# First head first in two attentions, small roots on GpSimd, a reordered opening, and whole-width blocks in the last feed-forward

## The chip, the cores and the metric

The kernel runs on one core of one Trainium2 chip. A core has five engines that run their own instruction lists side by side and wait for one another on semaphores: TensorE (PE, matrix multiplication, with its weight loads shown apart as PEld), VectorE (DVE), ScalarE (ACT), GpSimd (POOL) and SyncE (SP), which here issues nearly all transfers. Each engine works through its list in order. Matmul results go to PSUM, everything else lies in SBUF. The metric is the device time of one execution in microseconds.

## The reference

A backbone of two layers works on 512 latent tokens and 256 context tokens of width 1024, all in float32. In each layer a modulation vector (the "ada" products) scales and shifts the RMS norm of the tokens; one large projection feeds four mixers: A, attention in a window of tokens plus the context, B, dense attention with RMS-normed queries and keys, C, a gated recurrence in chunks (mLSTM), and D, a state-space scan in chunks (Mamba). Their outputs are projected back and added, and a feed-forward with squared relu follows. The last layer does not need the context's outputs.

```python
def attend(qblk, keys, vals, mask=None, sink=None):
    s = jnp.einsum('bqgrd,bkgd->bgrqk', qblk, keys)
    ...
def sq_relu_ffn(h, w1, w2):
    return jnp.square(jax.nn.relu(h @ w1)) @ w2
...
        x = x + gt1 * (jnp.concatenate([ya, yb, ym, yd], axis=-1) @ w_out[layer])
        h2 = rmsnorm(x, g_norm2[layer]) * (1 + sc2) + sh2
        x = x + gt2 * sq_relu_ffn(h2, w_ff1[layer], w_ff2[layer])
    return rmsnorm(x, g_final)
```

## The kernel before, in words

**Precision by splitting.** Each float32 operand of a large product is split into a rounded part and a remainder (h and hl, wh and wl, ah and al, yh and yl): ACT writes the rounded part, DVE the remainder, and three matmuls (high by high, high by low, low by high) make one product. The DVE and ACT work of most stages is this splitting. Line 96 is the helper of all plain matmuls, L107 of DVE's two-operand operations, L104 of ACT's, L112 and L115 of DVE's with scalars.

**Order of the work.** Latents are tokens 256 to 767 (LAT, 512 columns), the context the first 256 (CTX). The function walks through a layer stage by stage: projections, attention A, D, C, attention B, output projection, feed-forward. Stages of narrow or dependent matmuls are interleaved with wide ones by a stream of generators: `fill(t)` advances the stream by some work, and tables of numbers (FILL_A, FILL_D, FILL_C, FILL_CB) say how much stands at which place. A scheduler then orders each engine's instructions by when their inputs are modelled to be ready, so the order on an engine is not that of the program text. Tiles come from pools with a fixed number of buffers, and a new tile waits until the old one in its buffer is read.

**Opening (layer 0).** SP loads the tokens x in four pieces with constants (cst), per-column and per-row tables (pcol, prow) in between. ACT squares x, PE sums over partitions (ssq), four transposes and nine small DVE steps (`rsq`, a reciprocal root by a bit trick and two refinements) give the norm; PE spreads it to a row (prow_), ACT copies that to SBUF (rowx), and `norm_chunk` multiplies x by it (xn). `cond(q)` loads and multiplies the ada weights of the next columns; the wopen weights then feed the first projections.

**Attention.** `put_k` makes for each of two key heads a tile KHL with the rounded keys in one half of the partitions and the remainder in the other, for both: ACT rounds, DVE subtracts, DVE copies the rounded half across and ACT the remainder. `put_q` makes the query tiles EO, `rotate` applies the rotary embedding with two POOL multiplications and one on DVE (qs, ra), `v_ab` splits the values. `attend_s` makes the scores (tile s) of one unit, a key head and 128 queries, `attend_v` the products with the values. A has 12 units in layer 0 and 8 in layer 1, all of head 0 first. B in layer 0 does four query blocks of head 0, the same of head 1, then the other two; in layer 1 the heads alternate with each query block.

**Stage C and the start of B.** For each 128 tokens C makes raw products, an exponential mask (MB), the inter product with the state, the num product with the values (65 columns wide), and a norm over each head: ssC holds the squares' sums, `c_norm` takes their roots on DVE, `c_fin` multiplies on POOL (tho) and transposes. The stream at that time holds the projections of B's keys and queries: their squares (bsq) are summed by 2-column matmuls (`col_b`), `rsq_b` takes roots on DVE, `apply_k` multiplies the keys. For the last two blocks of tokens the norm and `c_fin` fall together with B's KHL and EO.

**Feed-forward.** Eight blocks b: `ffn1(b)` makes 512 hidden features, `ffn2(b - 1)` multiplies those of the block before back to 1024 and adds them to x. In layer 1 only the 512 latents count. Their inputs h2 are not normed: the two halves of 256 tokens are finished at different times, the norm's row is multiplied on DVE after the matmul, and two extra columns carry the shift (bs). So every product of `ffn1` is done in two parts, of 258 and 256 columns.

## Time and profile before

| | |
|---|---|
| median of 3 runs | 1825.8 us (1821.95 to 1827.46) |
| profiled execution | 1831.02 us |
| its span on the core | 1829.2 us |
| mean granted clock of TensorE | 0.981 |
| instructions | 31114 |
| POOL busy | 330.4 us, 332 instructions |
| bytes moved by the queue that the engines' transfers use | 176.88 MB |

A group of the profile names line, engine and operation, then the tile written, the tiles read, shapes and count, busy time and mean of one, and the idle time just before with the instruction that ended it. In the list of single instructions each row starts with time and duration, and the idle time before it stands in brackets. In the table by stretch of time the busy time of each engine is followed by the clock that the TensorE was granted (1.00 is full), the share of the DMA engines and GB/s.

### The profile page before, as it was taken

The page shows a single profiled execution, that of the slowest core. Times are in us where ns is not written, and L with a number is a line of the kernel's source. Part 1 is how long each engine was busy: PE and PEld are TensorE (multiplying, and loading weights), DVE is VectorE, ACT ScalarE, POOL GpSimd, SP SyncE. Part 2 cuts the span into 40 slices and gives each one's busy share as a digit, 9 for nine tenths or more (in the row PEclk, how much of TensorE's full clock was granted, in tenths as well). Part 3 has the DMA queues.
Part 4 walks back from the last instruction along what each step waited for, and adds up shares of the span by engine and source line. Part 5 has one row for each costly group of instructions (what it writes and reads, how often), then busy time and mean ns, then how long its engine had stood idle before and what let it go on. Part 6 is the DMA issues. An engine that isn't in the chain of part 4 may idle for free. (4 is left out here: it accounts for less than half of the span.)

```text
span 1829.2 us, 31114 instructions
## 1 busy us (share of the span) xinstructions
PE 1756.3 (96%) x11754; PEld 1541.2 (84%) x11754; DVE 1167.8 (64%) x2601; ACT 896.5 (49%) x1988; POOL 330.4 (18%) x332
## 2 busy tenths in 40 slices
PE   7999999989999999999999999999989999999997
...
GB/s 336 89 82 110 147 139 95 91 121 41 24 82 112 96 132 103 95 127 98 99 127 98 139 70 61 47 94 93 70 58 70 35 105 92 93 93 93 94 96 65
DMA packets 97685, 178.85 MB, mean 98 GB/s; under 512 B 10624, under 2 KB 19200, under 8 KB 97536
## 3 DMA queue, kind: packets, MB, share of 16 engines
q1 hardware_dynamic: 97536, 176.88, 30.1%
...
q14 instruction: 57, 0.47, 0.1%
...
## 5 line engine op out<-in xcount | busy, mean ns | idle before, releaser
L104 ACT ACTIVATE wh<-wraw 128x512 fp32r<-128x512 f32 (+1 forms) x392 | 238.4, 618 | 257.1 <-PE bulk L96 136.4
L107 DVE TENSOR_TENSOR wl<-wraw,wh 128x512 fp32r<-128x512 f32 (+1 forms) x392 | 281.9, 725 | 116.9 <-ACT wh L104 108.6
L96 PE MATMUL s<-h,wh 128*128 128x258 f32 (+2 forms) x1040 | 316.2, 313 | 1.1 <-ACT pr L104 1.1
L96 PE MATMUL s<-hl,wh 128*128 128x258 f32 (+2 forms) x1040 | 306.2, 313 | 0.0
L96 PE MATMUL s<-h,wl 128*128 128x258 f32 (+2 forms) x1040 | 252.5, 313 | 0.0
L96 PE MATMUL bulk<-ah,wh 128*128 128x512 f32 (+1 forms) x576 | 218.0, 378 | 3.9 <-DVE mod L107 3.2
L302 POOL TENSOR_TENSOR acc<-acc,adap 128x512 f32<-128x512 f32 x96 | 143.2, 1496 | 412.1 <-ACT acc L104 390.6
L96 PE MATMUL bulk<-ah,wl 128*128 128x512 f32 (+1 forms) x576 | 216.1, 375 | 0.0
L96 PE MATMUL bulk<-al,wh 128*128 128x512 f32 (+1 forms) x576 | 215.9, 375 | 0.0
L96 PEld LDWEIGHTS s<-h,wh 128*128 128x128 f32 x1040 | 197.0, 189 | 22.4 <-ACT pr L104 1.6
L115 DVE SCALAR_TENSOR_TENSOR x<-bulk,mod,x 128x512 f32<-128x512 f32 (+1 forms) x224 | 149.4, 671 | 103.3 <-PE bulk L96 102.2
L96 PEld LDWEIGHTS s<-hl,wh 128*128 128x128 f32 x1040 | 197.5, 190 | 11.8 <-issue 0.4
L96 PEld LDWEIGHTS s<-h,wl 128*128 128x128 f32 x1040 | 166.1, 190 | 1.1
L96 PE MATMUL bulk<-h,wh 128*128 128x512 f32 (+1 forms) x416 | 154.0, 370 | 3.8 <-DVE VS L107 2.3
L96 PE MATMUL bulk<-hl,wh 128*128 128x512 f32 (+1 forms) x416 | 144.8, 348 | 0.0
L96 PE MATMUL bulk<-h,wl 128*128 128x512 f32 (+1 forms) x416 | 144.5, 347 | 0.0
L96 PEld LDWEIGHTS bulk<-ah,wh 128*128 128x128 f32 x576 | 108.3, 188 | 24.9 <-DVE mod L107 4.9
L96 PEld LDWEIGHTS bulk<-ah,wl 128*128 128x128 f32 x576 | 108.2, 188 | 21.2
L96 PEld LDWEIGHTS bulk<-al,wh 128*128 128x128 f32 x576 | 108.3, 188 | 19.4
L104 ACT ACTIVATE relu<-relu,bs 128x512 f32<-128x512 f32 x96 | 58.8, 644 | 131.1 <-DVE relu L107 131.1
L104 ACT ACTIVATE adap<-adar,silw 128x256 f32<-128x256 f32 x192 | 85.2, 497 | 56.9 <-DMA adar<-in_wada_dram 52.6
L107 DVE TENSOR_TENSOR relu<-relu 128x512 f32<-128x512 f32 x96 | 88.1, 943 | 31.4 <-ACT relu L104 31.3
...
## 6 DMA issues: line engine op xcount, KB each, us to landing
wraw<-in_wf_dram SPq DMA_DIRECT2D x256, 256.0 KB, 2.7
...
```

Of the source, the lines that this page charges most:

```text
L96: return TE.matmul(o, lhsT=l, rhs=r, start=start, stop=stop)
L104: return S.activation(o, i, f, scale=scale, **kw)
L107: return V.tensor_tensor(o, a, b, op)
L115: return V.scalar_tensor_tensor(o, a, s, b, op0, op1)
L302: G.tensor_tensor(acc[:, v], acc[:, v], dst, ALU.add)
```

## The change

The change has six parts.

*Opening.* The four pieces of x are sent first, then cst and pcol; the first ada weights and wopen's first piece follow, the row tables and layer 1's pcol after them. The first two normalised chunks read the norm's row from PSUM, and its copy to SBUF comes behind them.

*First head first.* `put_k` takes a list of heads. In layer 0's A keys and queries of head 0 are rotated and split first; the values, head 1 and the context's queries follow. In B head 1's keys and queries follow the first unit. In layer 1 B's units alternate between the heads in pairs of query blocks. Where an attention has no scores made ahead, the same amount of stream work as behind the first scores also goes ahead of them.

*Copy by DMA.* For head 1 one POOL DMA copies rounded part and remainder across partitions instead of DVE and ACT.

*Roots on POOL.* `rsq` can run on POOL: eleven steps there, and the bit trick on DVE. C's norm and the norms of B's keys and queries use it; the last two `c_fin` multiply on DVE.

*Stage C.* The 2-column sums and the roots behind them wait in a list (mids) until the middle of the stream's next wide group. Both directions' weighted values (vw) are made before a common piece of stream work. The inter product directly follows raw, and a piece of stream work stands between the two halves of num.

*Feed-forward, layer 1.* While block 1 starts, `whole()` makes the normed latents in one piece: POOL multiplies x by the row, ACT scales and shifts, and the second 256 columns are split into h2's free columns; the first 256 follow at block 2. Blocks 2 to 7 then use 512-column matmuls, and the relu reads PSUM directly.

```diff
-    def load_cols(l):
-        SY.dma_start(pcs[l], pcol[l])
+    def load_row(l):
...
-        if q == 1:
-            SY.dma_start(cs, cst)
-        if q == 2:
-            load_cols(0)
+    SY.dma_start(cs, cst)
+    SY.dma_start(pcs[0], pcol[0])
...
-    def rsq(out_, src, scale, eps):
+    def rsq(out_, src, scale, eps, eng=V):
...
+        eng.tensor_scalar(v, src, scale, eps, ALU.mult, ALU.add)
         ts(y.bitcast(I32), v.bitcast(I32), -0.5, float(0x5F3759DF), ALU.mult, ALU.add)
...
+        eng.tensor_tensor(w, y, y, ALU.mult)
+        eng.tensor_tensor(w, w, v, ALU.mult)
+        if eng is V:
...
+        eng.tensor_scalar(t, w, -10.0 / 3.0, None, ALU.add)
+        eng.tensor_tensor(w, w, t, ALU.mult)
+        eng.tensor_scalar(w, w, 5.0, None, ALU.add)
+        eng.tensor_tensor(y, y, w, ALU.mult)
+        eng.tensor_tensor(w, y, y, ALU.mult)
+        eng.tensor_tensor(w, w, v, ALU.mult)
+        eng.tensor_scalar(w, w, -0.5 * 0.375 ** 3, 1.5 * 0.375, ALU.mult, ALU.add)
+        eng.tensor_tensor(out_, w, y, ALU.mult)
...
+            todo = mids.pop(0) if mids else None
             for k in range(len(W)):
+                if todo is not None and k == len(W) // 2:
+                    todo()
...
+            raws0 = [ada_load(i, (4, 0)[i]) for i in range(2)]
...
+            cond(0, raws0)
+            W0 = wload([wopen[i, 0] for i in range(2)])
+            for l_ in range(DEPTH):
+                load_row(l_)
+            SY.dma_start(pcs[1], pcol[1])
...
+                if q == 0:
+                    act(rows[i], prows[i], AF.Copy)
...
+        def put_k(src, khl_, sl, bs=(0, 1)):
+            for b in bs:
                 own = slice(64 * b, 64 * b + 64)
                 oth = slice(64 - 64 * b, 128 - 64 * b)
                 H, L = khl_[b][:, 0, sl], khl_[b][:, 1, sl]
                 act(H[own], src[own], AF.Copy)
                 tt(L[own], src[own], H[own].bitcast(F32), ALU.subtract)
-                V.tensor_copy(H[oth], H[own].bitcast(F32))
-                act(L[oth], L[own].bitcast(F32), AF.Copy)
+                if b:
+                    G.dma_start(khl_[b][oth, :, sl], khl_[b][own, :, sl])
+                else:
+                    V.tensor_copy(H[oth], H[own].bitcast(F32))
+                    act(L[oth], L[own].bitcast(F32), AF.Copy)
...
+            f = (stream.total - (first if head else 2 * first) - last) / nf
+            if head is None:
+                fill(first)
...
-            v_ab(pav[1], 0, 2)
-            put_k(pf[1][:, 0:256], khl["A"], CTX)
-            q_a(0, CTX, pf[1][:, 256:512])
-            put_k(rotate(pf[0][:, 0, :], None, tf((P, NL), name="ra"), rp), khl["A"], LAT)
-            q_a(0, LAT, pf[0][:, 1, :])
+            rk = rotate(pf[0][:, 0, :], None, tf((P, NL), name="ra"), rp)
+            put_k(pf[1][:, 0:256], khl["A"], CTX, (0,))
+            rq0 = rotate(pf[0][:, 1, :], None, tf((P, NL), name="ra"), rp)
+            put_k(rk, khl["A"], LAT, (0,))
+            put_q(rq0, eos["A", 0], LAT)
             for i in range(2):
                 v_ab(pav[0][:, i, :], 2 + 2 * i, 2)
+            v_ab(pav[1], 0, 2)
+            put_k(pf[1][:, 0:256], khl["A"], CTX, (1,))
+            put_k(rk, khl["A"], LAT, (1,))
+            q_a(0, CTX, pf[1][:, 256:512])
...
+                rsq(v, v, 1.0 / 64.0, EPS, G)
...
+        def later(*fs):
+            return g_do(lambda: mids.append(lambda: [f() for f in fs]), 0.4 * len(fs))
...
+        def cq(m):
+            return later(*[col_b(f"q{m}", sl, sqq) for sl in segs_q], rsq_b(f"q{m}", jq))
+
+        gs = [later(*[col_b("k", sl, sqk) for sl in (LAT, CTX)], rsq_b("k")), gq(0, LAT)]
+        gs += [gq(0, CTX)] if need else []
+        gs += [cq(0), g_do(apply_k(LAT), 0.5), g_do(apply_k(CTX), 0.5), gq(1, LAT)]
+        gs += [gq(1, CTX)] if need else []
+        gs += [cq(1)]
...
+                vws.append(vw)
+            fill(2 * wu * fC_)
+            for d in range(2):
+                j, vw = ORDERS[d][st], vws[d]
...
+            rsq(ssC[:, t4], ssC[:, t4], 1.0 / 64.0, EPS, G)
...
+            inter = s2()
+            for e in range(2):
+                for q in range(2):
+                    er = slice(64 * e, 64 * e + 64)
+                    mm(inter[:, e, q * 130:(q + 1) * 130], qT[er, q, js], SC[er, :, j, q, :])
...
+            fill((wa + 0.6 * wb) * fC_ if ji < nout - 1 else 1.5 * FILL_CB[l][4])
             num = s2()
             for e in range(2):
+                if e:
+                    fill(0.4 * wb * fC_ if ji < nout - 1 else 0.5 * FILL_CB[l][4])
...
-            put_k(kB[:, sl], khl["B"], sl)
+            put_k(kB[:, sl], khl["B"], sl, (0,))
...
+        for sl in segs_out:
+            put_q(qB[:, 0, sl], eos["B", 0], sl)
+        units = [(kv, j) for js_ in ((out_tok[:4], out_tok[4:]) if need else (out_tok[:2], out_tok[2:])) for kv in range(2) for j in js_]
...
+            c_fin(j, V)
...
         def done_b(kv, j):
+            if (kv, j) == units[0]:
+                for sl in (LAT, CTX):
+                    put_k(kB[:, sl], khl["B"], sl, (1,))
+                for sl in segs_out:
+                    put_q(qB[:, 1, sl], eos["B", 1], sl)
...
+        def whole():
+            for c in range(8):
+                t = T((P, NL), F32, "ada", 4, "xn") if c % 2 == 0 else ta((P, NL), name="xn")
+                nrm.append(t)
+                G.tensor_tensor(t, xr[c // 2][:, c % 2, LAT], rowt[0], ALU.mult)
+                act(t, t, AF.Identity, scale=sc2[0][:, c:c + 1], bias=md[:, 0, 24 + c:25 + c])
+                put_whole(c, 1)
+
+        def put_whole(c, i):
+            dst = slice(NE + 256 * i, NE + 256 * i + 256)
+            split_act(nrm[c][:, 256 * i:256 * i + 256], h2[c][0][:, dst], h2[c][1][:, dst], slice(0, 256))
...
+            full = not need and b >= 2
...
+                sg = [(0, slice(NE, NE + NL))] if full else psegs
+                if full:
+                    ks = [(m, [0], k) for m in range(2) for k in range(8)]
...
+                    if full:
+                        act(r[:, LAT], o[:, 0, :], AF.Relu)
+                        tt(r[:, LAT], r[:, LAT], r[:, LAT], ALU.mult)
+                        split_act(r[:, LAT], ah, al, LAT)
+                        continue
...
+            if not need and b == 1:
+                whole()
+            if not need and b == 2:
+                for c in range(8):
+                    put_whole(c, 0)
```

The scheduler's order shows where it moves instructions. SP in the opening (x, cc, cst are tokens, condition and constants, adaw and wraw weights), before:

```order
L133 DMA x_66<-in_xin_dram 128x1536
L137 DMA cst_63<-in_cst_dram 128x386
L133 DMA x_67<-in_xin_dram 128x1536
L129 DMA pcol_69<-in_pcol_dram 128x102
L130 DMA prow_71<-in_prow_dram 128x40
L133 DMA x_68<-in_xin_dram 128x1536
L232 DMA adaw_189<-in_wada_dram 128x1024
L232 DMA adaw_199<-in_wada_dram 128x1024
L232 DMA adaw_216<-in_wada_dram 128x1024
L232 DMA adaw_226<-in_wada_dram 128x1024
```

and with the change:

```order
L132 DMA x_66<-in_xin_dram 128x1536
L132 DMA x_67<-in_xin_dram 128x1536
L132 DMA x_68<-in_xin_dram 128x1536
L135 DMA cst_63<-in_cst_dram 128x386
L136 DMA pcol_69<-in_pcol_dram 128x102
L241 DMA adaw_101<-in_wada_dram 128x1024
L241 DMA adaw_103<-in_wada_dram 128x1024
L241 DMA adaw_105<-in_wada_dram 128x1024
L241 DMA adaw_107<-in_wada_dram 128x1024
L176 DMA wraw_241<-in_wopen_dram 128x512
L176 DMA wraw_247<-in_wopen_dram 128x512
L129 DMA prow_71<-in_prow_dram 128x40
```

The constants and the first pcol now stand behind the fourth x, the row table prow behind the first ada and wopen weights.

DVE at the start of A in layer 0 (KHL_797 is head 0's keys, KHL_798 head 1's, EO_799 head 0's queries, ra rotated tiles, VS values), before:

```order
L107 TENSOR_TENSOR ra_829<-s_56_186,rope_793 128x512
L107 TENSOR_TENSOR VS_796<-s_54_184,VS_796 128x2x2x64
L107 TENSOR_TENSOR EO_799<-bulk_187,EO_799 64x256 x2
L107 TENSOR_TENSOR KHL_797<-ra_829,KHL_797 64x512
L628 CAST KHL_797<-KHL_797 64x512
L107 TENSOR_TENSOR KHL_798<-ra_829,KHL_798 64x512
L628 CAST KHL_798<-KHL_798 64x512
L107 TENSOR_TENSOR ra_846<-s_56_186,rope_793 128x512
L107 TENSOR_TENSOR wl_1021<-wraw_1026,wh_1020 128x280
L107 TENSOR_TENSOR EO_799<-ra_846,EO_799 64x512 x2
```

and with the change, where KHL, EO and VS keep their numbers:

```order
L107 TENSOR_TENSOR ra_813<-s_60_191,rope_793 128x512
L107 TENSOR_TENSOR KHL_797<-bulk_192,KHL_797 64x256
L659 CAST KHL_797<-KHL_797 64x256
L107 TENSOR_TENSOR VS_796<-s_58_189,VS_796 128x2x2x64
L107 TENSOR_TENSOR wl_994<-wraw_999,wh_993 128x280
L107 TENSOR_TENSOR ra_826<-s_60_191,rope_793 128x512
L107 TENSOR_TENSOR KHL_797<-ra_813,KHL_797 64x512
L659 CAST KHL_797<-KHL_797 64x512
L107 TENSOR_TENSOR KHL_798<-bulk_192,KHL_798 64x256
L107 TENSOR_TENSOR EO_799<-ra_826,EO_799 64x512
L107 TENSOR_TENSOR KHL_798<-ra_813,KHL_798 64x512
L107 TENSOR_TENSOR EO_799<-ra_826,EO_799 64x512
```

Head 1's two copies (CAST) are gone, its splits stand behind head 0's keys, and the second rotation (the queries') comes ahead of head 0's latent keys.

DVE at the start of B in layer 0, from the last sum of C's norm (ssC) on (rv, ry, rw are steps of its root, KHL_4863 is head 1's keys, EO_4880 and EO_4881 are head 0's queries; head 0's keys stand farther ahead), before:

```order
L1385 TENSOR_REDUCE ssC_4053<-sqc_4788 128x4
L107 TENSOR_TENSOR KHL_4863<-kB_3671,KHL_4863 64x512
L112 TENSOR_SCALAR rv_4792<-ssC_4053 128x8
L628 CAST KHL_4863<-KHL_4863 64x512
L112 TENSOR_SCALAR ry_4793<-rv_4792 128x8
L107 TENSOR_TENSOR KHL_4863<-kB_3671,KHL_4863 64x256
L107 TENSOR_TENSOR rw_4794<-ry_4793 128x8
L628 CAST KHL_4863<-KHL_4863 64x256
L107 TENSOR_TENSOR rw_4794<-rw_4794,rv_4792 128x8
L107 TENSOR_TENSOR EO_4880<-qB_3672,EO_4880 64x512
L115 SCALAR_TENSOR_TENSOR rw_4794<-rw_4794 128x8
```

and with the change (rg is the root's tile on POOL, m the maximum of the first scores, EO_4875 and EO_4876 head 0's queries):

```order
L1429 TENSOR_REDUCE ssC_4051<-sqc_4790 128x4
L107 TENSOR_TENSOR EO_4875<-qB_3670,EO_4875 64x256
L112 TENSOR_SCALAR rg_4794<-rg_4794 128x8
L107 TENSOR_TENSOR EO_4876<-qB_3670,EO_4876 64x256
L107 TENSOR_TENSOR wl_4979<-wraw_4980,wh_4978 128x512
L721 TENSOR_REDUCE m_916_4886<-s_918_4888 128x1
L721 TENSOR_REDUCE m_916_4886<-s_920_4897 128x1
L115 SCALAR_TENSOR_TENSOR m_916_4886<-m_916_4886,rq_792 128x1
L1376 TENSOR_TENSOR tho_3668<-tho_3668,ssC_4051 128x256
L115 SCALAR_TENSOR_TENSOR m_916_4886<-m_916_4886,rq_792 128x1
L115 SCALAR_TENSOR_TENSOR x_4646<-bulk_4829,mod_89,x_4646 128x512
L1376 TENSOR_TENSOR tho_3668<-tho_3668,ssC_4051 128x256
```

Of the root one step is left on DVE; head 1's splits stand farther behind, and the multiplications of tho (L1376) with additions to x behind them have come to DVE.

92 lines of the change are left out of this document (35 added, 57 removed).

## The prediction

> **What bounds the kernel now.** I read the page first, for the busy shares:
>
> ```profile
> PE 1756.3 (96%) x11754; PEld 1541.2 (84%) x11754; DVE 1167.8 (64%) x2601; ACT 896.5 (49%) x1988; POOL 330.4 (18%) x332
> ```
>
> TensorE (PE) is the bound, and the other engines matter where they stop it. Two things can be gained: time in which PE stands still, and time in which it works slowly. The table by stretch of time shows both; the columns are busy time of PE, PEld, DVE, ACT, POOL, then the granted clock.
>
> ```profile
> 28.00:84.00 56.00, 55.94 (x530) 48.66 (x531) 30.75 (x73) 31.29 (x70) 11.71 (x10) 0.97 0.47 155
> 84.00:94.00 10.00, 6.24 (x26) 4.97 (x25) 7.08 (x12) 7.71 (x16) 5.18 (x4) 0.66 0.36 108
> 320.00:364.00 44.00, 43.19 (x286) 35.82 (x286) 26.32 (x75) 20.02 (x48) 11.64 (x13) 0.84 0.31 95
> 364.00:394.00 30.00, 29.12 (x206) 24.69 (x205) 22.98 (x67) 15.99 (x29) 8.68 (x9) 0.83 0.43 138
> 394.00:412.00 18.00, 12.01 (x58) 9.59 (x57) 15.65 (x37) 8.91 (x23) 2.39 (x3) 0.81 0.24 79
> 1320.00:1354.00 34.00, 32.98 (x195) 27.02 (x194) 27.29 (x79) 20.70 (x39) 9.26 (x9) 0.95 0.23 71
> 1354.00:1376.00 22.00, 15.24 (x58) 11.41 (x58) 20.04 (x54) 9.35 (x23) 3.59 (x5) 0.84 0.23 79
> 1498.50:1771.00 272.50, 272.50 (x1730) 247.15 (x1729) 148.03 (x242) 90.83 (x145) 0.00 (x0) 1.00 0.30 94
> ```
>
> From such a row I take two upper bounds: standing time, the length less PE's busy time, and clock loss, the length times (1 − clock). 84 to 94 (A's start in layer 0): 3.8 and 3.4. 320 to 394 (stage C, layer 0): 1.7 and 12.1. 394 to 412 (B's start, layer 0): 6.0 and 3.4. 1320 to 1354 (C, layer 1): 1.0 and 1.7. 1354 to 1376 (B's start, layer 1): 6.8 and 3.5. Clock loss counts idle time too, so the two overlap. From 1498 on PE is full at full clock; only less work shortens that.
>
> **The feed-forward of layer 1.** The chain of waits alternates blocks of the first product (tile s) with blocks of the second (bulk):
>
> ```profile
> 1520.60 23.16 PE s L96 x192
> 1543.76 22.30 PE bulk L96 x96
> 1566.05 23.16 PE s L96 x192
> 1589.21 22.20 PE bulk L96 x96
> 1747.58 23.12 PE s L96 x192
> ```
>
> Both do the same arithmetic, but the first as 192 matmuls of 256 and 258 columns, since the two halves of the tokens are normalised at different times and each half carries extra columns. The change gives blocks 2 to 7 a finished 512-column input, so they become 96 matmuls of 512 columns, the bulk form: 23.15 − 22.25 = 0.9 us each, six blocks, **−5.6 us** (−5 to −6). The relu then reads PSUM without the row multiplication, so DVE has less to do.
>
> The price is the new input. Right after block 0's inputs, POOL multiplies eight 128x512 tiles, ACT shifts and rounds them, DVE takes the rest. POOL's nearest rows:
>
> ```profile
> L302 POOL TENSOR_TENSOR acc<-acc,adap 128x512 f32<-128x512 f32 x96 | 143.2, 1496 | 412.1 <-ACT acc L104 390.6 <-ACT adap L104 18.6
> L606 POOL TENSOR_TENSOR qs<-qs,rope 128x512 f32<-128x512 f32 x12 | 15.7, 1306 | 142.5 <-ACT qs L104 142.5
> L1333 POOL TENSOR_TENSOR tho<-tho,ssC 128x256 f32<-128x256 f32 x10 | 7.1, 731 | 23.6 <-DVE ssC L115 23.6
> L1013 POOL MEMSET v<- 128x24 f32 x2 | 0.3, 142 | 44.1 <-PE s L96 44.1
> ```
>
> Eight at 1.31 to 1.50 us are 10.5 to 12.0 us, and ACT, in order, follows them. Queued behind on ACT is block 1's weight rounding, needed for these matmuls:
>
> ```profile
> L104 ACT ACTIVATE wh<-wraw 128x512 fp32r<-128x512 f32 (+1 forms) x392 | 238.4, 618 | 257.1 <-PE bulk L96 136.4
> 1461.08 0.39 ACT L104 ACTIVATE row<-mx 128x256 f32<-128x256 f32 x1 [4.46 <-PE mx L96]
> 1475.06 0.29 PE L96 MATMUL s<-h,wh 128*128 128x258 f32 x1
> ```
>
> The row exists at 1461.5, so POOL is through at 1472.0 to 1473.5, and ACT's last pair plus the first weights (0.62 + 0.39 + 0.62) land at 1473.6 to 1475.1, against a need at 1475.1. Bounds 0 and +3 (if DVE's subtractions queue too); I take **+1.0**. The second half of this input is rewritten under a 22 us bulk block by 8 × 0.39 = 3.1 us of ACT and as much of DVE: nothing.
>
> **The opening.**
>
> ```profile
> 4.00:8.00 4.00, 1.87 (x8) 0.40 (x8) 0.59 (x4) 2.43 (x4) 0.00 (x0) 1.00 1.03 403
> 8.00:12.00 4.00, 4.00 (x17) 0.75 (x16) 0.51 (x4) 2.41 (x4) 0.00 (x0) 1.00 0.66 244
> 14.43 1.57 ACT L104 ACTIVATE sq<-x 128x768 f32<-128x768 f32 x2 [1.73 <-DMA x<-in_xin_dram]
> 24.67 0.87 ACT L104 ACTIVATE rowx<-s 128x512 f32<-128x512 f32 x2 [2.29 <-PE s L96]
> 25.30 1.42 DVE L115 SCALAR_TENSOR_TENSOR xn<-x,sc,rowx 128x512 f32<-128x512 f32 x2 [1.87 <-ACT rowx L104]
> 28.06 0.39 PE L96 MATMUL s<-wh,h 128*128 128x256 f32 x1 [1.71 <-ACT h L104]
> ```
>
> Constants and two tables of small packets stand ahead of the fourth x, and the transfers sag from 403 to 244 GB/s in 8 to 12 us. The change sends all four x first: at 403 GB/s the 159 GB/s missing for 4 us are 1.6 us, and cst (0.2 MB) is 0.5. x then lands 2.1 us sooner, more if the weights behind it also share less. The normalisation multiplies straight from PSUM (0.63 us of copying off the path), and the row's matmuls go ahead of an ada transpose (some 0.7). The first projection moves by 3.4 or more; afterwards PE has no idle to absorb it (55.94 of 56 us). Bounds −1.6 (all that follows tied to the transfers) and −5; I take **−3.5**.
>
> **Attention A.** Before, both heads' keys were split, copied across partitions by DVE and ACT, and the values split too, ahead of the first scores:
>
> ```profile
> 82.72 0.63 ACT L104 ACTIVATE KHL<-KHL 64x512 fp32r<-64x512 f32 x1
> 88.17 1.22 PE L96 MATMUL s<-KHL,EO 128*128 128x512 f32 x2 [3.76 <-DVE EO L107]
> 1120.87 0.50 PE L96 MATMUL s<-KHL,EO 128*128 128x512 f32 x1 [1.50 <-DVE EO L107]
> ```
>
> Layer 0 now rotates keys and queries first, prepares head 0 alone, and sends head 1's copy by two POOL DMAs. On ACT head 1's rounding and its copy, 0.63 each, no longer stand between the query's rotation and its split, and the values' splits, about as long together, partly move behind too: 2.5 of the 3.8 us, and with so short a stall 1.5 of the 3.4 us of clock loss. Bounds −1 (POOL's part of the rotation, 2 × 1.31, stays) and −7.2 (both whole); I take **−4.0**. In layer 1 the prologue gets an equal filling before the first scores, taken out of later ones: **−1.2**, bounds 0 and −1.5. Head 1's copy has many attention units before its first reader.
>
> **Stage C.** Here PE hardly stands but is slowed:
>
> ```profile
> 345.00:349.90 4.90, 4.45 (x40) 4.31 (x38) 2.60 (x7) 4.78 (x13) 3.38 (x5) 1.00 0.11 28
> 349.90:360.10 10.20, 10.20 (x39) 7.60 (x38) 5.72 (x14) 3.56 (x12) 2.85 (x4) 0.50 0.21 52
> 373.80:384.00 10.20, 9.60 (x58) 7.32 (x58) 8.78 (x31) 6.19 (x13) 1.50 (x1) 0.50 0.79 252
> 348.39 1.05 PE L96 MATMUL bulk<-cst,bsq 128*128 128x2 f32 x8 [0.45 <-DVE qB L115]
> ```
>
> Half clock comes after runs of narrow matmuls (2 and 65 columns) with stalls below 1 us. The change hangs the 2-column sums into the middle of a wide group, moves the inter products up and puts wide work between the halves of num. That may cost one window of 10.2 us, worth at most 5.1, or none. Bounds +2 (narrow runs meet elsewhere) and −8; I take **−2.5** for both layers.
>
> The Trainium skill, "TensorE: Matmul & The Clock Gate", section "Why this matters for your kernels", asks for no PE-idle gaps over about 3 us. By it breaking narrow runs wins nothing, and only the 3.76 us stall matters. The trace disagrees: the window at 349.9 follows no such gap. By the rule the sum is 2.5 us smaller, which the third rival contains.
>
> **Attention B.** Layer 0, where DVE runs the root of C's norm (9 steps) and the eight key and query splits in turn, and PE waits for all of it:
>
> ```profile
> 396.58 0.17 DVE L112 TENSOR_SCALAR rv<-ssC 128x8 f32<-128x8 f32 x1
> 397.24 0.17 DVE L112 TENSOR_SCALAR ry<-rv 128x8 int32<-128x8 int32 x1
> 402.47 0.17 DVE L115 SCALAR_TENSOR_TENSOR ssC<-rw,ry 128x8 f32<-128x8 f32 x1
> 399.45 1.87 PE L96 MATMUL s<-KHL,EO 128*128 128x384 f32 x8 [1.00 <-DVE EO L107]
> 403.88 0.44 PE L1336 MATMUL mx<-cst,tho 128*128 128x128 f32 x2 [1.97 <-POOL tho L1333]
> 407.50 0.58 PE L96 MATMUL bulk<-yh,wh 128*128 128x256 f32 x1 [2.18 <-DVE x L115]
> ```
>
> The root takes 402.64 − 396.58 = 6.1 us there. After the change head 1's splits come after the first unit, and the root is 11 steps on POOL with one on DVE. No row has a small arithmetic step on POOL. Below: MEMSET 128x24, 0.14 us; above: tho 128x256, 0.73. From 128x256 to 128x512 a multiplication grows by 0.58 us; taken back to 24 elements that leaves 0.21, near the MEMSET. I take 0.21: 12 × 0.21 + 0.2 for two changes of engine = 2.7 us, 3.4 less than now. New wait: DVE's multiplication of tho waits for POOL, and behind it in DVE's order stand additions to x that free PE's PSUM. With about 3 us of DVE work between, that wait is short. Head 1's copies (POOL DMAs) are read several units later in layer 0, two in layer 1.
>
> Of the 6.0 us standing and the half clock after it I take **−4.0** in layer 0 and **−4.0** in layer 1 (6.8 standing), each with bounds +3 (the 0.73 step) and −8. Roots for k and q go to POOL likewise, under wide feature groups.
>
> The Trainium skill, "GPSIMD Engine Reference", section "Key points", holds VectorE structurally about twice as fast at elementwise work. By that, twice DVE's 0.17, the root would take 12 × 0.34 = 4.1 us instead of 2.7, and the gain in B would shrink by some 1.4 us in each layer. No run shows it yet.
>
> **Sum.** −5.6 + 1.0 − 3.5 − 4.0 − 1.2 − 2.5 − 4.0 − 4.0 = −23.8. The profiled execution took 1831.0 us: 1807.2. It lies 5.2 above the median of 1825.8, so at the median 1802.0. Some waits will move rather than vanish: I leave 2 us for that and forecast **1804 us**.
>
> **Rivals.** *Only the firm parts land* (0.22). Feed-forward (−4.6 with its price) and opening (−3.5) count, A by half (−2.6); C and B find new waits as long as the old: −10.7, 1815. For it: DVE is busy 15.65 of 18 us in B's start and the work is only reordered. Against: 6 us of standing there comes from an order that the change undoes.
>
> *POOL's roots become the bound* (0.06), the slower side. With steps of 0.73 us a root is 12 × 0.73 = 8.8 us. It decides from 6.1 / 12 = 0.5 us a step, where it takes longer than today's. At 0.73, B loses its 8.0 and pays 2.7 a layer: +13.4. Three roots a layer for k, q0 and q1 grow from 9 × 0.17 = 1.5 to 8.8, by 7.3; a half feature group (12 matmuls of 22.3 / 96 = 0.23, 2.8) covers part, 4.5 stays, times six +27. 1804 + 13 + 27 = 1844; with four of the six covered, 1826, and with three 1831. Against: the sizes are 2 to 16 elements, not 256.
>
> *The clock stays low* (0.12). Stalls go, but the narrow runs and a shorter stall still halve the clock: C's 2.5 and the clock share of A and B (half of 3.4, 3.4 and 3.5) are missing, 7.7 us: 1812.
>
> *It doesn't do what it says* (0.03): x lands no sooner and head 1's copies come late, +3.5 and +2 × 2.5: 1812.
>
> **How the numbers follow.** The forecast has 0.57, its own range 1796 to 1811. Bounds of all terms reach 1790 and 1830; leaving out a tenth below and a tenth above, where only the first rival's tail and POOL's lie, gives 1793 to 1818. What this kernel's times can tell from no change is about 0.3%, 5.5 us: faster means under 1820.3. The main case and the two rivals at 1812 hold that nearly whole, the first rival for four fifths: 0.87 faster. The rest of these, and a part of POOL's case, is 0.08 within; 0.05 slower.
>
> **What would show it.** Right: s blocks of x96 and 22.3 us in the chain; first projection matmul near 24.5; no 3.76 us wait for EO; B's stretches 5 us shorter; POOL's small steps near 0.2 us. Wrong: small POOL steps of 0.5 us or more with DVE's tho behind them; PE waiting for weights at block 1 of layer 1; half-clock windows as long as before.

## The result, and the profile after

The changed kernel takes **1814.57 us** (median of 5 runs, 1809.93 to 1815.62), the kernel before 1827.46 us (1821.95 to 1832.36) in the same comparison. The ratio is 0.9911, 95% interval 0.9888 to 0.9935: faster by 0.9%, more than the 0.3% that the prediction took as noise, and with the whole interval below 1. Between the medians lie 12.9 us, between the two profiled executions 17.0 us (1831.02 and 1813.98), since the one before lies above its median. The forecast was 1804, a gain of 21.8 us; the time lies in the range of 1793 to 1818, but above the likeliest case's own 1796 to 1811. Direction and order of size were right; the terms were not, and some failed.

The page of the changed kernel, its busy shares and its DMA queues:

```profile
PE 1737.6 (96%) x11178; PEld 1505.2 (83%) x11178; DVE 1158.1 (64%) x2485; ACT 900.8 (50%) x2004; POOL 372.5 (21%) x454
q0 software_dynamic: 1152, 1.57, 0.5%
```

PE has 576 instructions less (six blocks, 96 each), POOL 122 more, and a queue appears for POOL's copies of head 1's keys. PE's busy time falls by 18.7 us, its span by 17.0: the time in which PE stands still has not shrunk at all. Six blocks of the feed-forward account for 4.5 us of this, and up to 9.4 us are clock: the mean granted clock rose from 0.981 to 0.986 (0.019 × 1829.2 − 0.014 × 1812.2, the missing share of the clock times the span).

The same stretches of the program in both profiled executions show where the 17.0 us come from. A stretch runs from the start of one named PE row to the start of another; the last column is the difference.

| stretch | before, us | changed, us | difference |
|---|---|---|---|
| start to first projection matmul | 28.06 | 23.22 | −4.84 |
| to A's last scores, layer 0 | 168.55 | 168.38 | −0.17 |
| to C's first transpose, layer 0 | 98.60 | 96.84 | −1.76 |
| C and B to the last product with yS, layer 0 | 227.22 | 217.43 | −9.79 |
| feed-forward, layer 0 | 551.89 | 553.18 | +1.29 |
| to D's first transpose, layer 1 | 143.74 | 145.41 | +1.67 |
| to C's first transpose, layer 1 | 71.77 | 73.24 | +1.47 |
| C and B to the last product with yS, layer 1 | 164.42 | 161.01 | −3.41 |
| to block 0's second product, layer 1 | 43.97 | 47.00 | +3.03 |
| rest of that feed-forward | 318.67 | 314.14 | −4.53 |
| to the end | 12.35 | 12.36 | +0.01 |

The stretches to C's first transpose have nearly no edit in them and differ by −1.8 and +1.5; so much a single profile can show from nothing (the last section says why). Differences of 3 us and more I take for findings. The five kernels whose C and B are those of the changed kernel (it and four of the experiments) put a measure on that: 217.1 to 218.9 us in layer 0, 159.1 to 161.6 in layer 1.

The opening and the start of A in layer 0, transfers by time first (last columns: clock, share of the DMA engines, GB/s), then PE:

```profile
8.00:12.00 4.00, 4.00 (x20) 0.75 (x16) 0.32 (x3) 3.35 (x6) 0.00 (x0) 1.00 1.03 411
23.22 0.39 PE L96 MATMUL s<-wh,h 128*128 128x256 f32 x1 [2.12 <-ACT h L104]
79.88 0.74 PE L96 MATMUL s<-KHL,EO 128*128 128x512 f32 x2 [1.56 <-DVE EO L107]
82.28 0.37 PE L96 MATMUL bulk<-wh,h 128*128 128x280 f32 x1 [1.66 <-DVE EO L107]
```

The sag to 244 GB/s is gone and the first projection is 4.84 us sooner. A's single wait of 3.76 us has become two of 1.56 and 1.66.

Stage C and the start of B, layer 0 then layer 1, by time:

```profile
312.00:355.00 43.00, 39.55 (x294) 33.14 (x289) 24.92 (x62) 19.83 (x47) 13.60 (x24) 0.92 0.30 92
355.00:370.70 15.70, 15.65 (x150) 13.83 (x150) 12.92 (x25) 11.74 (x21) 12.31 (x29) 1.00 0.32 107
370.70:396.00 25.30, 19.99 (x113) 17.54 (x113) 20.92 (x47) 13.29 (x31) 10.37 (x27) 0.93 0.44 150
1298.00:1336.00 38.00, 32.62 (x208) 27.27 (x207) 23.91 (x52) 21.92 (x41) 17.09 (x43) 0.91 0.15 50
1336.00:1358.00 22.00, 19.52 (x100) 15.29 (x100) 19.11 (x42) 9.92 (x24) 10.44 (x27) 0.92 0.20 62
```

Clocks of 0.81 to 0.84 have become 0.92 to 1.00 in layer 0, but PE now stands 3.5, 5.3, 5.4 and 2.5 us in four of these stretches (length less PE's busy time; 0.05 in the second). In layer 1 one wait is new, and the rows of DVE, POOL and PE show its cause:

```profile
1328.76 0.20 POOL L192 TENSOR_SCALAR rg<-kcq 128x8 f32<-128x8 f32 x1 [2.83 <-DVE kcq L1192]
1334.09 0.20 POOL L211 TENSOR_TENSOR kcq<-rg 128x8 f32<-128x8 f32 x1
1334.32 0.17 DVE L111 TENSOR_SCALAR rq<-kcq 128x8 f32<-128x8 f32 x1 [3.68 <-POOL kcq L211]
1335.08 0.68 DVE L107 TENSOR_TENSOR yc<-yc,s 128x512 f32<-128x512 f32 x1
1335.90 1.20 PE L96 MATMUL s<-SC,qT 64*128 64x130 f32 x8 [3.08 <-DVE yc L107]
```

Two roots, of the queries and of C's norm, take turns on POOL from 1328.76 to past 1334.09, some 5.5 us. DVE waits for the first with C's yc behind it, and PE waits for yc.

The feed-forward of layer 1, two blocks from the chain of waits, and then the rows at its one wait:

```profile
1619.76 22.29 PE bulk L96 x96
1642.04 22.35 PE s L96 x96
```

```profile
1446.00 12.72 POOL L1515 TENSOR_TENSOR xn<-x,row 128x512 f32<-128x512 f32 x8 [3.76 <-ACT row L104]
1451.23 1.75 DVE L107 TENSOR_TENSOR wl<-wraw,wh 128x512 fp32r<-128x512 f32 x1
1452.90 1.51 DVE L107 TENSOR_TENSOR hl<-xn,h 128x256 fp32r<-128x256 f32 x1
1453.04 0.39 PE L96 MATMUL s<-h,wl 128*128 128x258 f32 x1 [2.29 <-DVE wl L107]
```

Blocks of x96 at 22.4 us, as forecast, but DVE's subtractions take 1.5 to 1.75 us while POOL multiplies, and PE waits 2.29 us for one of them.

### The profile page after: what moved, and what is told of

The parts are those of the page before. It is cut to its first block, busy times and chain, and to the rows that moved or that the text cites. A ratio compares the mean times of both kernels' runs of the same rounds, so it can differ in the third digit from the quotient of the medians.

```text
span 1812.2 us, 29981 instructions
## 1 busy us (share of the span) xinstructions
PE 1737.6 (96%) x11178; PEld 1505.2 (83%) x11178; DVE 1158.1 (64%) x2485; ACT 900.8 (50%) x2004; POOL 372.5 (21%) x454
## 4 chain that ended last, share of the span: by engine, by line
PE 75%; DVE 7%; ACT 5%; POOL 5%; DMA 4%; issue 3%; SPq 0%; POOLq 0%; ACTq 0%; DVEq 0%
PE bulk L96 36%; PE s L96 29%; PE mx L96 8%; PE mx L757 2%; DMA MB<-drows 1%; DVE wl L107 1%; ACT qs L104 1%; POOL acc L317 1%; DMA adar<-in_wada_dram 1%; ACT wh L104 1%; DMA CB<-drows 1%; DVE x L115 1%; POOL qs L633 1%; DVE m L721 0%; ACT pr L104 0%
## 5 line engine op out<-in xcount | busy, mean ns | idle before, releaser
L107 DVE TENSOR_TENSOR wl<-wraw,wh 128x512 fp32r<-128x512 f32 (+1 forms) x392 | 288.3, 742 | 138.4 <-ACT wh L104 130.6
L96 PE MATMUL s<-h,wh 128*128 128x512 f32 (+2 forms) x848 | 291.7, 346 | 1.1 <-ACT pr L104 1.1
L96 PE MATMUL s<-hl,wh 128*128 128x512 f32 (+2 forms) x848 | 281.6, 345 | 0.2 <-DVE hl L115 0.2
L96 PE MATMUL s<-h,wl 128*128 128x512 f32 (+2 forms) x848 | 251.3, 346 | 2.3 <-DVE wl L107 2.3
L96 PEld LDWEIGHTS s<-h,wh 128*128 128x128 f32 x848 | 160.5, 189 | 30.8 <-ACT pr L104 1.5
L96 PEld LDWEIGHTS s<-hl,wh 128*128 128x128 f32 x848 | 160.6, 189 | 20.1 <-DVE hl L115 0.4
L96 PEld LDWEIGHTS s<-h,wl 128*128 128x128 f32 x848 | 142.9, 190 | 12.6 <-DVE wl L107 2.8
L96 PE MATMUL bulk<-wh,h 128*128 128x256 f32 (+1 forms) x304 | 92.9, 306 | 4.3 <-DVE EO L107 1.7
```

What stands on the lines that cost most here:

```text
L96: return TE.matmul(o, lhsT=l, rhs=r, start=start, stop=stop)
L107: return V.tensor_tensor(o, a, b, op)
```

## The experiments

All ratios are to the kernel before, timed on the same chip in the same session, with 95% intervals; the changed kernel's is 0.9911 (0.9888 to 0.9935). 0.001 is 1.8 us. Since one profile wanders by some microseconds where nothing was edited, I read ratios for totals and the stretches above for places. Most intervals of single edits overlap the changed kernel's, so most of these experiments can only be read by place.

### Which term of the making of the whole input costs

The whole input's multiplications moved from POOL to DVE:

```diff
-                G.tensor_tensor(t, xr[c // 2][:, c % 2, LAT], rowt[0], ALU.mult)
+                tt(t, xr[c // 2][:, c % 2, LAT], rowt[0], ALU.mult)
```

> The changed kernel, but the eight 128x512 multiplications that make the whole normed input run on DVE instead of POOL, in the same place. Contention theory: in the changed kernel PE waits 2.29 us for wl because DVE's subtractions on two SBUF operands take 1.5 to 1.8 us instead of 0.4 to 0.7 while POOL multiplies. Without POOL they take 0.4 to 0.7 again; DVE gets 8 x 0.69 = 5.5 us of multiplications but saves more, the wait falls below 1 us, and the stretch from the row (1445.5) to the first block of the second product (1485.7), 40.2 us, falls to about 38: total 2 us less than the changed kernel. Queue theory: the wait comes from work queued ahead of block 1's weights, whoever multiplies; with 5.5 us more on DVE it stays at 2.3 us or grows, and the stretch is 40 to 43 us.

Ratio 0.9894 (0.9866 to 0.9922). The stretch from the last product with yS to block 0's second product falls from 47.00 to 44.07 us (before: 43.97). The chain and the rows of DVE in this kernel:

```profile
1449.78 37.44 PE s L96 x310
1487.22 22.21 PE bulk L96 x96
1452.06 0.68 DVE L107 TENSOR_TENSOR wl<-wraw,wh 128x512 fp32r<-128x512 f32 x1
1455.73 0.42 DVE L107 TENSOR_TENSOR hl<-xn,h 128x256 fp32r<-128x256 f32 x1
```

The first block runs in 37.44 us without a wait, as in the kernel before:

```profile
1461.04 37.34 PE s L96 x310
```

The subtractions take 0.68 and 0.42 us. DVE carries 5.5 us more and is still done in time. Contention was the cause, not the queue; the repair takes 2.9 us out of that stretch, more than the expectation's 2. In all seven kernels that keep POOL's multiplications the stretch is 46.97 to 48.06 us, in the others 43.92 to 44.08. The ratio points the same way (3.1 us), but its interval overlaps the changed kernel's.

The same with the work written behind block 1's first product:

```diff
-            if not need and b == 1:
-                whole()
...
             at = ffn1(b)
+            if not need and b == 1:
+                whole()
```

> As the run with DVE's multiplications, but they and the splits behind them are written after block 1's first product, to run under the second product of block 0. Both theories: no wait at block 1's weights, the stretch from the row to the first block of the second product is 37.2 us as in the kernel before. Open is whether DVE has room under the 22.2 us of the second product: it is busy 12.5 us in such a block, and 5.5 + 16 x 0.42 = 12.2 us come on top. If it fits, 3 us less than the changed kernel; if not, PE waits some 2 us for block 2's input and the gain is 1 us.

Ratio 0.9902 (0.9869 to 0.9934); the stretch is 43.92 us, the rest of the feed-forward 314.12. It fits under the second product, and gives nothing beyond the first repair.

No whole input at all, with `full = False` and without the calls:

```diff
-            full = not need and b >= 2
+            full = False
```

> The changed kernel without the whole-width input: all blocks of layer 1's first product stay in two parts, 192 matmuls each. By my account the six blocks gain 6 x 0.75 = 4.5 us and the making costs 3.0, so this kernel should be 1.5 us slower than the changed one (some 1811.5 against 1813.98 of span times reversed: 1815.5 in the profiled time), not the 4.6 us that the prediction gave. If the making cost nothing after all, it is 4.5 us slower.

(Its bracket mixes span and time; the 1.5 us stand.) Ratio 0.9909 (0.9888 to 0.9931), the same as the changed kernel within the interval. The stretches are 43.92 and 318.71 against 47.00 and 314.14: the six blocks win 4.57 us and the making costs 3.08, 1.5 us net. In the other kernels that keep POOL's multiplications the making costs up to 4.1. With the multiplications on POOL, then, a term that the prediction counted among its firm parts is worth some 0.5 to 1.5 us; with the multiplications on DVE it is worth 4.4.

### What the roots on POOL are worth

All roots on DVE:

```diff
-                rsq(v, v, 1.0 / 64.0, EPS, G)
+                rsq(v, v, 1.0 / 64.0, EPS)
...
-            rsq(ssC[:, t4], ssC[:, t4], 1.0 / 64.0, EPS, G)
+            rsq(ssC[:, t4], ssC[:, t4], 1.0 / 64.0, EPS)
```

> The changed kernel with all roots of stage C and of B's norms on DVE again (nine steps), the last two multiplications of tho still on DVE. Theory that POOL's roots cost: in layer 1 two root chains interleave on POOL for 5.5 us, DVE waits 3.68 us for the factor rq with C's multiplication behind it, and PE stands 3.1 us; in layer 0 DVE waits 1.2 and 0.7 us. On DVE these waits go: 3 to 5 us less than the changed kernel between C's start and B's first scores of layer 1, and 1 us in layer 0. Prediction's theory (POOL takes the load off DVE): DVE gets five roots of 1.8 us a layer back in its busiest stages, and the kernel is 2 to 5 us slower.

Ratio 0.9903 (0.9880 to 0.9927): by time not told from the changed kernel. By place layer 0 is: C and B take 212.94 us there (217.43 changed), and PE stands 9.9 us instead of 13.3 in it. The changed kernel, then the one with all roots on DVE:

```profile
288.44:505.87 217.43, 204.14 (x1487) 177.67 (x1488) 162.64 (x398) 118.21 (x269) 36.33 (x79) 0.98 0.22 68
291.37:504.31 212.94, 203.08 (x1488) 175.75 (x1489) 165.57 (x438) 117.83 (x269) 21.69 (x24) 0.98 0.22 69
```

Layer 1 takes 158.87 us (161.01); that lies only 0.3 below the lowest kernel with POOL's roots (159.1), so its 2.1 us may be nothing. The roots on POOL cost, they don't relieve, though not where the theory looked: it gave 1 us to layer 0 and 3 to 5 to layer 1. In layer 1 C itself shrinks from 64.89 to 56.88 us, and 4.6 of that come back in B, where PE stands 5.3 us instead of 2.9.

Only the factor rq on POOL as well, so that DVE needn't wait for it:

```diff
-                    ts(rq[:, j0:NJ, 2 * m:2 * m + 2], kcs[n][:, j0:NJ, :], 0.125, None, ALU.mult)
+                    G.tensor_scalar(rq[:, j0:NJ, 2 * m:2 * m + 2], kcs[n][:, j0:NJ, :], 0.125, None, ALU.mult)
```

> The changed kernel with one step more on POOL: the factor rq of the queries' norm is multiplied by POOL and not by DVE, so DVE does not wait for POOL's root with C's multiplication yc behind it. If this wait is what the roots on POOL cost, the 3.08 us for yc in layer 1 (near 1332 us) goes, and 1.2 us of DVE's waiting in layer 0: 3 to 4 us less than the changed kernel in C and B, as much as with all roots on DVE in layer 1. If the cost lies in the roots' length on POOL (4.3 us alone, 5.5 in pairs), the wait moves to the next reader, the multiplication of tho or the first scores' exponential, and less than 1 us is won.

Ratio 0.9907 (0.9877 to 0.9938). C in layer 1 shrinks by 5.2 us, from 64.89 to 59.70, but C and B together stay at 161.21 (161.01), and 216.56 in layer 0 (217.43). The wait for yc goes and returns later, as the second theory had it: taking away the waiting instruction alone wins less than 1 us. That theory's reason, the roots' length, is not borne out. With all roots on DVE the four roots of the queries take 4.2 to 7.2 us from first step to last, with other work of DVE between the steps; on POOL, in the changed kernel, they take 3.3 to 5.5.

Only C's norm on DVE, the roots of B's keys and queries on POOL, and the whole input on DVE:

```diff
-            rsq(ssC[:, t4], ssC[:, t4], 1.0 / 64.0, EPS, G)
+            rsq(ssC[:, t4], ssC[:, t4], 1.0 / 64.0, EPS)
```

> The repaired kernel (whole input's multiplications and all roots on DVE) with the roots of B's keys and queries back on POOL; only the roots of C's norm stay on DVE. Both kinds run on POOL at once in layer 1, where DVE waited 3.68 us. If C's norm is what must not be on POOL (two chains side by side, and tho waits for it), this kernel keeps the gain: from C's start to the output products 213 to 214 us in layer 0 and 159 in layer 1, ratio 0.986 to 0.988. If the queries' roots are the cost (DVE's factor rq waits, C's multiplication behind it), it falls back to 216 to 217 and 161, ratio 0.989 to 0.990.

Ratio 0.9908 (0.9887 to 0.9929), C and B 217.34 and 163.66 us: it falls back. DVE's list of waits in this kernel (us in total, times, longest):

```profile
DVE rq L111 <- POOL kcq L211: 7.6, 4, 2.4
DVE kR L1209 <- POOL kck L211: 3.0, 1, 3.0
```

These are the two rows that the changed kernel has as well (7.8 and 3.0 us), and they are absent in the kernel with all roots on DVE. The roots of B's keys and queries are costly by themselves; C's norm alone on POOL was not run. DVE, which works in order, stands in these rows, but that the roots cost by this is argued, not shown: the kernel with rq on POOL lacks the longer row and wins nothing by the end of B. A wait for the keys' root (kR, 3.1 us there) remains in it.

### Both repairs together

> The changed kernel with two repairs: the whole input's multiplications on DVE, and all roots on DVE. From the runs with one repair each: 3.0 us less from the row to the first block of layer 1's second product, 4 to 5 us less from C's start to the output products in layer 0, 2 to 3 in layer 1; if they add, 8 to 10 us less than the changed kernel, a ratio to the kernel before of 0.986. If the roots' waits merely move when DVE is loaded, as half of them did in layer 1, 5 us and 0.989.

The whole input's multiplications and all roots are on DVE, the edits of the first and the fourth kernel above. Ratio **0.9865** (0.9834 to 0.9896), median 1807.95 us with the kernel before at 1832.72. C and B take 213.84 and 158.79 us, the stretch of the whole input 44.07: by place the repairs add. It lies 0.0046 below the changed kernel's ratio, 8.4 us, as expected, though the two intervals overlap by 0.0008. Each repair alone gave less by ratio, 3.1 and 1.5 us. The kernel that differs from it only in the roots of B's keys and queries has 0.9908.

### What each other part is worth

The opening alone, on the kernel before (x first, the row tables late, the normalised chunks from PSUM):

> The kernel before with the reordered opening alone. If the opening's gain is its own, the first projection matmul starts near 23.2 us, as in the changed kernel, and not at 28.06, and everything behind it keeps that distance: 4.5 to 5 us less than the kernel before, give or take half-clock windows of 1.7 us each. Rival: the opening only pulls forward a start that the ada and wopen transfers then hold back; PE would idle later in the stretch to the first scores (60.1 us in the kernel before), and 1.6 us or less would remain.

Ratio 0.9980 (0.9961 to 0.9999), 3.7 us, with 0.2 to 7.1 possible. The first projection starts at 23.28 us:

```profile
23.28 0.58 PE L96 MATMUL s<-wh,h 128*128 128x256 f32 x1 [2.11 <-ACT h L104]
```

The stretch to the first scores behind it grows from 60.11 to 61.51 us, so 1.4 of the 4.78 us may be lost, the size that clock windows make of nothing.

A's start as before:

```diff
-            rk = rotate(pf[0][:, 0, :], None, tf((P, NL), name="ra"), rp)
-            put_k(pf[1][:, 0:256], khl["A"], CTX, (0,))
...
+            v_ab(pav[1], 0, 2)
+            put_k(pf[1][:, 0:256], khl["A"], CTX)
...
-            if head is None:
-                fill(first)
```

> The changed kernel with the start of attention A as in the kernel before: values, both heads' keys and the context's queries in the old order in layer 0 (head 1's copies still by DMA), and in both layers no stream work ahead of the first scores. From the first projection to the last scores of A in layer 0 took 168.55 us in the kernel before and 168.38 in the changed one. Theory that the wait only moved, since PE asks for the scores 3.5 us sooner and then waits 1.6 us before and 1.7 us behind them: that stretch stays at 168 to 170 us, and the total within 1.5 us of the changed kernel's. The prediction's theory, that 4.0 and 1.2 us were won: 172 us there, and the total 5 us more.

Ratio 0.9919 (0.9895 to 0.9943), 1.5 us slower and within the interval. The stretch from the first projection to A's last scores is 170.72 us; ten kernels with the new start and the new opening have 168.37 to 171.70. In layer 1 the stretch to D's first transpose is 143.20 (new: 143.55 to 145.56). By half clock (the last section) the kernels can be paired more closely. With 6.8 us of it at the start of the projections and none near 147 us, four kernels with the new start take 169.28 to 169.49 us, and the two with the old start behind the new opening 170.20 and 170.72. A's new start is worth some 1 us, which the ratio can't tell from nothing.

Head 1's copies by DVE and ACT:

```diff
-                if b:
-                    G.dma_start(khl_[b][oth, :, sl], khl_[b][own, :, sl])
-                else:
-                    V.tensor_copy(H[oth], H[own].bitcast(F32))
-                    act(L[oth], L[own].bitcast(F32), AF.Copy)
+                V.tensor_copy(H[oth], H[own].bitcast(F32))
+                act(L[oth], L[own].bitcast(F32), AF.Copy)
```

> The changed kernel with head 1's keys copied across by DVE and ACT again instead of by POOL's DMAs. The copies stand behind the first unit now, so nothing waits for them in either form: DVE gets 0.42 + 0.29 us and ACT 0.63 + 0.42 us back per attention and layer, under PE's work. Theory: within 1 us of the changed kernel. If DMA's relief was worth something (the prediction's reading of ACT's queue at A's start in layer 0), 1 to 2 us slower, with the stretch from the first projection to A's last scores in layer 0 above 170 us.

Ratio 0.9904 (0.9881 to 0.9927): no difference. A's stretch is 170.22 us, inside what the other kernels show. The copy by DMA neither helps nor hurts.

Stage C's order as before:

```diff
-            inter = s2()
-            for e in range(2):
-                for q in range(2):
-                    er = slice(64 * e, 64 * e + 64)
-                    mm(inter[:, e, q * 130:(q + 1) * 130], qT[er, q, js], SC[er, :, j, q, :])
...
-            fill((wa + 0.6 * wb) * fC_ if ji < nout - 1 else 1.5 * FILL_CB[l][4])
+            fill(wa * fC_ if ji < nout - 1 else FILL_CB[l][4])
+            inter = s2()
...
-                if e:
-                    fill(0.4 * wb * fC_ if ji < nout - 1 else 0.5 * FILL_CB[l][4])
```

> The changed kernel with stage C's order as before: 2-column sums where they were, one weighted value at a time, inter behind the first filling, num in one run; roots still on POOL, B's start still by heads. Theory that runs of narrow matmuls bring half clock: from C's start to the last output product of layer 0 (217 us with the change, 227 before) 4 to 7 us come back, with half-clock windows of 17 us or more together in 320 to 375 us. Theory that only waits above some 3 us count for the clock and that the gain there is B's: 0 to 2 us come back.

Ratio 0.9964 (0.9949 to 0.9979): 9.7 us of the gain are gone, and the interval is apart from the changed kernel's. C and B take 220.20 us in layer 0 (+2.8, between the 4 to 7 and the 0 to 2 of the two theories) and 165.99 in layer 1 (+5.0). The stretches of layer 0, C up to the last product of its numerators and then B up to its last scores, and the same two of layer 1, in the kernel with the old order:

```profile
290.60:378.70 88.10, 86.40 (x706) 73.96 (x707) 45.23 (x120) 40.15 (x89) 29.55 (x64) 0.92 0.29 92
378.70:482.70 104.00, 97.17 (x599) 84.78 (x599) 89.55 (x212) 60.24 (x139) 6.44 (x16) 0.98 0.20 60
1280.50:1345.30 64.80, 61.55 (x442) 50.86 (x442) 35.20 (x88) 30.22 (x60) 19.93 (x52) 0.95 0.19 64
1345.30:1411.30 66.00, 61.09 (x333) 50.95 (x333) 58.60 (x128) 39.34 (x85) 8.77 (x19) 0.97 0.23 71
```

And in the changed kernel:

```profile
288.40:370.70 82.30, 78.79 (x690) 68.38 (x690) 45.84 (x116) 39.12 (x87) 25.91 (x53) 0.96 0.28 89
370.70:477.70 107.00, 99.30 (x617) 87.24 (x617) 91.70 (x217) 61.30 (x141) 10.42 (x27) 0.98 0.21 68
1277.70:1342.60 64.90, 59.52 (x443) 50.81 (x442) 37.70 (x84) 29.85 (x59) 21.66 (x46) 0.92 0.19 61
1342.60:1405.00 62.40, 59.50 (x333) 49.38 (x333) 57.56 (x130) 39.85 (x86) 7.15 (x26) 1.00 0.23 71
```

In layer 0 the new order makes C 5.8 us shorter. The clock's part is 0.08 × 88.1 − 0.04 × 82.3 = 3.7 us; the rest is wide work moved behind C (16 matmuls fewer in it, 18 more behind), less 1.8 us that PE stands longer in C; B is 3.0 us longer. This much holds in every kernel: with the new order C of layer 0 has 3.4 to 10.2 us at half clock (eleven kernels), with the old order 13.7 to 23.9 (three). In layer 1 C itself gains nothing; what follows it is 3.6 us shorter, with the same 333 matmuls: PE stands 2.9 us there instead of 4.9 (length less busy time), and 0.03 of the clock on 66 us is 2.0 more, together about the 3.6. So most of layer 1's gain lies in B, behind C. Why the order of C shortens that is argued, not shown: the new order puts more filling into C's last block of tokens, and DVE and POOL have more time before PE wants their results. Of the ratio's 9.7 us the places account for 7.8.

That half clock comes without a long stall is seen in C of layer 0 in the old order. PE's list of waits there begins with

```profile
PE bulk L96 <- ACT qB L104: 0.9, 1, 0.9
```

so the longest is 0.9 us, and still 8% of the clock is gone. That the narrow runs bring it rests on the comparison of the two orders, in which wide work moved as well.

B's start as before (both heads ahead of the first scores, tho on POOL):

```diff
-            put_k(kB[:, sl], khl["B"], sl, (0,))
+            put_k(kB[:, sl], khl["B"], sl)
...
-        for sl in segs_out:
-            put_q(qB[:, 0, sl], eos["B", 0], sl)
+        for m in range(2):
+            for sl in segs_out:
+                put_q(qB[:, m, sl], eos["B", m], sl)
...
-            c_fin(j, V)
+            c_fin(j)
```

> The changed kernel with the start of attention B as before: both heads' keys and queries split ahead of the first scores, the old order of units in layer 1, the last two multiplications of tho on POOL; roots still on POOL, head 1's copies still by DMA, stage C as changed. The prediction gave B's start 8.0 us in both layers together, the account of the stretches so far leaves it 0 to 3 us, since stage C's order alone is worth 8 to 10 of the 13. If the prediction's size holds, this kernel is 6 to 8 us slower than the changed one (ratio to the kernel before about 0.995); if the account holds, 0 to 3 us (0.991 to 0.993).

Ratio 0.9948 (0.9927 to 0.9969), 6.8 us slower, as the prediction's size had it; my later account was too low. C and B take 223.40 and 167.16 us, 6.0 and 6.2 more. In layer 1 PE's waits at B's start:

```profile
1358.14 0.94 PE L96 MATMUL s<-KHL,EO 128*128 128x384 f32 x4 [2.73 <-DVE EO L107]
1365.13 0.69 PE L1379 MATMUL mx<-cst,tho 128*128 128x128 f32 x2 [4.20 <-POOL tho L1376]
```

The same two places in the kernel before:

```profile
1364.09 0.41 PE L96 MATMUL s<-KHL,EO 128*128 128x384 f32 x1 [2.08 <-DVE EO L107]
1367.64 0.33 PE L1336 MATMUL mx<-cst,tho 128*128 128x128 f32 x1 [1.70 <-POOL tho L1333]
```

With C's root on POOL and the multiplication of tho on POOL behind it, the second wait is 2.5 us longer than there, so the old order suffers more from POOL's roots than the new. By place the new start is worth 12.1 us, by the ratio 6.8 (the profiled execution, 1827.10 us, lies 4 us above its kernel's median, and the two intervals overlap by 0.0008), and either holds only beside those roots. The edit undoes three things at once, the heads' order ahead of the scores, the order of units and the engine of tho; what each is worth was not run.

Taken one by one, the gains come to more than the whole. By ratios the opening gives 3.7, C 9.7 and B 6.8, the feed-forward 1.5 net by place: 21.7. POOL's roots take 6.6 by place, which leaves 15.1; the changed kernel's own ratio gives 16.3. Each ratio is uncertain by 3 to 4 us, so this agrees in size and shows no more.

## Why the prediction was right or wrong

**Opening: right, a little more.** −3.5 forecast, −4.84 at the first projection, 3.7 us by the ratio of the opening alone. The shares came out otherwise than worked out. The transfers kept 411 GB/s, and ACT was through with the squares of x at 12.73 us instead of 16.00: 3.3 us, where the sum had 2.1. The row's matmuls start at 17.65 instead of 23.03, another 2.1 us: 0.8 because ada work of PE no longer stands between the root and them (the sum had 0.7), and 1.3 because the sums of squares run at full clock, where the kernel before had half clock from 15.4 to 22.2 us (the sum had nothing for it). Behind the row nothing was won, where the sum had 0.63 for the copy: from the row's matmuls to the first projection it is 5.57 us, 5.03 before. The copy left the path, but an ada transpose that ran ahead of the row now stands behind it, and DVE's first step with the row waits for its result.

**Feed-forward blocks: right mechanism, a fifth too large.** −5.6 forecast, −4.5 measured in every kernel with whole blocks (314.12 to 314.14 against 318.67 to 318.72). The s blocks take 22.4, not 22.25, so 0.75 us each, not 0.9. (Six times 0.9 is also 5.4, not the 5.6 in the sum. A second slip is in the range: the lower bounds as stated add to −43.7, which is 1782 at the median and not 1790.)

**The price of the whole input: too small by a factor of three or four, and for a reason left out.** Forecast was +1.0, measured 3.0 to 4.1. The step "ACT's last pair plus the first weights ... land at 1473.6 to 1475.1" reckoned POOL's time and ACT's queue. The wait came from DVE: its operations on two SBUF operands ran 1.5 to 1.8 us beside POOL, instead of 0.4 to 0.7. The upper bound of +3 just about held it in the changed kernel (3.03), and for DVE ("if DVE's subtractions queue too"), but not because they queue. The kernel before showed it already, in a group that I had not read by shape:

```profile
L107 DVE TENSOR_TENSOR relu<-relu 128x512 f32<-128x512 f32 x64 | 60.2, 941 | 31.4 <-ACT relu L104 31.3
```

A mean of 941 ns is a mixture: the 32 of layer 1, without POOL's additions, have a mean of 0.69 us, the 32 of layer 0 one of 1.19.

**Attention A: wrong in size, −5.2 forecast, some 1 us measured.** The step "2.5 of the 3.8 us, and with so short a stall 1.5 of the 3.4 us of clock loss" took the readiness of head 0's tiles for PE's gain. The scores are 3.45 us sooner, but that much wide work now stands behind them instead of ahead, and PE waited 1.56 us for the first scores and 1.66 right behind them, 3.2 in place of 3.76. The clock's share of the step came in part: half clock at A's start went from 6.8 us, in all three kernels with the old start, to 0 to 3.4 in ten of the eleven with the new. POOL plays in there too: while it rotates, DVE's copy of head 0's keys, in the second of these rows, takes 1.39 us:

```profile
76.76 1.61 POOL L638 TENSOR_TENSOR ra<-ra,qs 128x512 f32<-128x512 f32 x1
77.26 1.39 DVE L659 CAST KHL<-KHL 64x512 fp32r<-64x512 f32 x1
```

A copy of the same size took 0.42 in the kernel before:

```profile
80.95 0.42 DVE L628 CAST KHL<-KHL 64x512 fp32r<-64x512 f32 x1
```

In layer 1 no run shows a gain either.

**Stage C: the sign right, the size too small.** −2.5 forecast with bounds +2 and −8; undoing it costs 9.7 us by time and 7.8 by place. Less half clock after narrow runs was the right mechanism in layer 0, 3.7 us there. What the term left out lies behind C: in layer 1 B is 3.6 us shorter with the new order of C, and I had counted nothing for C outside C.

**Attention B: the size right, the roots wrong.** −8.0 forecast. Its new order is worth 6.8 us by the ratio, and the first scores of layer 0 wait for nothing (no bracket in the row):

```profile
385.32 0.34 PE L96 MATMUL s<-KHL,EO 128*128 128x384 f32 x1
```

But "12 × 0.21 + 0.2 ... = 2.7 us" for POOL's root was too low (the other estimate beside it, 4.1, came nearer, though by steps of 0.34), and "roots for k and q go to POOL likewise, under wide feature groups", which the sum put at nothing, was the step that failed. The rows of POOL:

```profile
386.26 0.42 POOL L192 TENSOR_SCALAR rg<-ssC 128x8 f32<-128x8 f32 x1 [1.54 <-DVE ssC L1429]
387.49 0.64 POOL L196 TENSOR_TENSOR rg<-rg 128x8 f32<-128x8 f32 x1
389.14 0.20 POOL L207 TENSOR_TENSOR rg<-rg 128x8 f32<-128x8 f32 x1
390.31 0.20 POOL L211 TENSOR_TENSOR ssC<-rg 128x8 f32<-128x8 f32 x1
```

A step is 0.20 to 0.25 us, as estimated, but the next starts 0.28 to 0.3 after it, the first ones take up to 0.64, and the root takes 390.51 − 386.26 = 4.25 us, 5.5 where two share POOL. That is the rival "POOL's roots become the bound" at a sixth of its price (6.6 us of the 40 between 1844 and 1804), without the 0.5 us a step that it asked for: DVE's reader of the root stands in order ahead of other DVE work, which waits with it. That this wait is the whole cost is not shown (above). The roots cost 4.5 us in layer 0 and at most 2.1 in layer 1. The kernel with both repairs, of the roots and of the whole input, has a median of 1807.95 us, near the forecast.

**The sum.** −23.8 less 2 for moved waits was forecast, −17.0 came in the profiled executions. The opening (1.3 us more) and C and B (−13.2 together for −10.5) beat their terms; A (5.0 less, its layer 1 stretch counted below), the whole input (2.0) and the blocks (1.1) fell short. The four other stretches (−1.8, +1.3, +1.7 and +1.5) add 2.7, which I count as what a single profile shows from nothing: −23.8 − 1.3 − 2.7 + 5.0 + 2.0 + 1.1 + 2.7 = −17.0.

The first rival, "only the firm parts land", gave 1815 and came nearest to the time, yet by its account it was wrong: of its firm parts the feed-forward gave a third, and what it wrote off, C and B, gave the most. That the forecast's range held is in part luck: A's missing 5 us and the whole input's 2 were partly made up for by C, B and the opening.

**The clock rule.** The prediction weighed a rule of the Trainium skill, "TensorE: Matmul & The Clock Gate", section "Why this matters for your kernels", that gaps above 3 us matter. By that rule stage C's order would not touch the clock; C of layer 0 in the old order has 0.92 with no wait above 0.9 us, the new order 0.96 with one of 1.5, so in this case staying below such gaps was not enough to keep full clock.
